# Output projection in three units, rotary in two operations, tables in 12, x from two queues: a two-layer encoder on one Trainium2 core

## The chip, the cores and the metric

The kernel runs on one core of one Trainium2 chip. The metric is the device time of one execution in microseconds (us), as the median over runs. The engines are TensorE (PE, matmuls and transposes, with a separate row PEld for its weight loads), VectorE (DVE), ScalarE (ACT), GpSimd (POOL) and SyncE (SP), which here only issues DMA transfers.

## What is computed

The reference, cut to the two layers that run (DEPTH is 2; SEQ is 512, D_MODEL 1024, 16 heads of 64, D_FF 4096):

```python
h = x
for i in range(DEPTH):
    y = rms_norm(h, norm1[i])
    y = mixer_a(y, ...) if i == 0 else mixer_b(y, ...)
    h = h + y
    h = h + jnp.square(jax.nn.relu(rms_norm(h, norm2[i]) @ w1[i])) @ w2[i]

def mixer_a(h, w_qkv, q_gain, k_gain, w_o, cos, sin):        # dilated attention
    qkv = (h @ w_qkv).reshape(B, S, 3, 3, 16, 64)            # 3 groups: dilation 1, 4, 16, radius 64, 64, 64
    for g in range(3):
        q = partial_rope(rms_norm(qkv[:, :, g, 0], q_gain[g]), cos, sin)   # rotary on 16 of 64 columns
        k = partial_rope(rms_norm(qkv[:, :, g, 1], k_gain[g]), cos, sin)
        num, den, mx = dilated_group(q, k, qkv[:, :, g, 2], dil, radius)
    ...                                                      # the groups are joined by their row maxima
    return (num / den) @ w_o

def mixer_b(h, w_in, conv_w, w_out):                         # gated convolution of width 3
    b, c, xt = split(h @ w_in); return (b * conv(c * xt)) @ w_out
```

## The kernel before

Every product is made in three matmuls: each float32 operand is split into a rounded high part and the remainder, and high x high, high x low and low x high are added in PSUM. A weight block of 128 rows (one k-block) is loaded by SP into `wraw` (4 buffers), ACT casts its high part `wh` (L292), POOL subtracts the remainder `wl` (L293; 6 buffers of each). The first two blocks of all are split by DVE (L959, L960).

The order of the work is written by a small planner. `add_unit` makes a unit of matmuls, cut into k-blocks; a clock counts its size, and one unit of that clock is the work of 12 matmuls of 512 columns. `at(pos, fn)` puts a task on a heap, and the run loop (L969 to L978) emits the tasks whose position has been passed between two matmuls. Each engine then runs its instructions in exactly that order, and waits at one hold up all behind it. For the attention the table `PLACES` gives the positions: its first row for pair 0, the second for pairs 1 to 6, the third for pair 7, the last.

**Start.** `setup` (L201) loads x into the tiles sm0 and sm12 (named sm in the profile), 128 columns by 128 columns at first and then 256 by 256, two transfers each (L198, L199), all issued by SP, with the weight blocks of the first four k-blocks between them. On ACT's queue stands the load of the norm gains (L203), then the table load and a first Exp (L214). `xT_fill` (L298) transposes x by PE (L301); ACT writes hgh, the high part with the gain applied (L305), and a copy to oT (L306), from which DVE makes the low part hgl (L307). PE's first matmul of the projection (L128) needs hgh of k-block 0. The copies of x transposed in oT go out to a DRAM buffer xs (L660).

**Layer 0, attention.** The 16 heads are 8 pairs. For each pair three units of 384 columns project q, k and v of the three groups. Two of them are evacuated to rawA and rawB (four tiles each, one for each residue r). Then come squares and sums (L364), the reciprocal root in ten small DVE operations (L367, L151 to L157), and `norm_mul` (L371): one multiplication by the root (L373) and the rotary in four operations (L379 to L382), on DVE or POOL as the table says. `qk_fill` transposes the result (L391) and splits it with the gains in `cols` (L405, L407). `tables` (L244) makes the cos and sin tables with the gains, tabA and tabB, in 48 small DVE operations (L254, L255) from loaded constants; `gain_cols` (L258) transposes the gain vectors to `cols` (L262, L263). Scores, softmax, the joining of groups by `spread` and `swap` (L428, L437), transposes (L520) and PV (L548) follow; ACT and DVE add both halves into oT (L551, L552).

**Output projection.** `split_o` splits oT into the tiles hgh and hgl of hgA. Two units of 512 columns (four tiles of 128 output columns each), over all eight k-blocks, are added to the trunk tiles hT, which `open_trunk` (L682) loads back from xs when the first tile is done; `wo_done` adds (L749), and `new_h` (L693) makes the high and low part for the next product (L705, L706) and the sum of squares (L707, L704). The last tile's oT is complete only after the last PV of pair 7; the last k-block of the first unit stands by itself, and its split at 1.0 units before that unit's end.

**The rest.** The MLP (L785), the gated convolution and a second MLP run with PE almost without a pause. The last additions of the last MLP (L817) go through a buffer zr (two of them), from which SP and ACT send the result out (L818, L819).

Of the kernel before, what the change touches and what calls it, by code (L numbers as in the profile page):

```python
# [11 lines left out]
F32 = mybir.dt.float32  # L12
# [23 lines left out]
def _constants():  # L36

    c = np.arange(128)
    r = np.arange(4)
    t = 4 * _C2M[:, None] + r[None, :]  # L40
    inv = (500000.0 ** (-np.arange(0, 16, 2) / 16.0)).astype(np.float32)
    ang = (t.astype(np.float32)[..., None] * inv).astype(np.float32).astype(np.float64)
    cos, sin = np.cos(ang), np.sin(ang)
    rope = np.concatenate([cos, cos, -sin, sin], axis=-1).astype(np.float32)
    m0 = np.zeros((128, 3, 256), np.float32)
    p = np.arange(128)
    for n, b in enumerate((0, 1, 3)):
        tq = 4 * _C2M[32 * b + p % 32] + p // 32
        tk = np.concatenate([4 * _C2M[_KEYC[j]] + _KEYR for j in ((b - 1, b) if b else (0, 3))])
        m0[:, n] = np.where(np.abs(tq[:, None] - tk[None, :]) <= 64, 0.0, BIG)  # L50
    m12 = np.zeros((128, 2, 128), np.float32)
    dm = _C2M[:, None] - _C2M[None, :]
    m12[:, 0] = np.where(np.abs(dm) <= 64, 0.0, BIG)
    m12[:, 1] = np.where(dm % 4 == 0, 0.0, BIG)
    return {"rope": rope.reshape(128, 4, 32), "m0": m0, "m12": m12.reshape(128, 256)}
# [7 lines left out]
         dN=0.04, P=11.9, dP=0.6, gP=0.5, lP=1.6, qA=0, qB=0, pA=0, pB=3, pN=2, vA=0, vB=8, xq=3.57, dxq=0.29, xs=6.25,  # L63
         lg=2.48, dlg=0.43, tb=5.8, dtb=0.3, gc=8.63),
# [10 lines left out]
def trunk_kernel(ctx, tc, x, norm1, norm2, wqkv, qgain, kgain, wo, win, conv, wout, w1, w2, c_rope, c_m0, c_m12, out):  # L75
# [119 lines left out]

    def load_x(lo, hi):
        dst = xtile[lo // 512][:, :, lo % 512:lo % 512 + hi - lo]
        sync.dma_start(dst[16:128], xr[0:112, :, lo:hi])  # L198
        sync.dma_start(dst[0:16], xr[112:128, :, lo:hi])  # L199

    def setup():  # L201
        vec = ptile(ab, [16, 128], F32, "vec", tag="tmpO")
        act.dma_start(vec, norm1.rearrange("l (k c) -> (l k) c", c=128))  # L203
# [10 lines left out]
        act.activation(small[:, 12:13], ident[:, 0:1], AF.Exp)  # L214
# [29 lines left out]
    def tables(ty):  # L244
        need("gains", 0, 3)
        mark("tables", 0)
        gb, rope = box["gb"], box["rope"]
        dst, w = (tabA, ty) if ty < 3 else (tabB, ty - 3)
        g = gb[:, ty % 2, ty // 2]
        for h in range(2):  # L250
            for a in range(2):
                s = slice(8 * a, 8 * a + 8)
                o = slice(8 * (1 - a), 8 * (1 - a) + 8)
                dve.tensor_mul(dst[:, 0, :, w, h, s], rope[:, :, s], g[:, None, s].to_broadcast([128, 4, 8]))  # L254
# [116 lines left out]
    def norm_mul(raw, stt, ng, tab, r, eng):  # L371
# [7 lines left out]
        eng.tensor_mul(t1[:, :ng], rot, tb[:, 0, r])  # L379
        eng.tensor_mul(t2[:, :ng, 0:8], v[:, :, 8:16], tb[:, 1, r, :, 0:8])  # L380
        eng.tensor_mul(t2[:, :ng, 8:16], v[:, :, 0:8], tb[:, 1, r, :, 8:16])
        eng.tensor_add(rot, t1[:, :ng], t2[:, :ng])  # L382

# [357 lines left out]

    def wo_done(half):
        def f(n, ps):
            if half == 0 and n == 0:
                for k in ("vp", "attn"):
                    close_pool(k)
                open_trunk()
            h = state["hT"][4 * half + n]
            dve.tensor_add(h, ps, h)  # L749
            new_h(4 * half + n, G2)  # L750
            if half == 1 and n == 3:
                for k in ("hgA", "oT", "psM0", "psG"):
                    close_pool(k)
                state["psM"] = open_pool("psM", space=PSUM, bufs=8)
        return f

# [28 lines left out]
    def mlp(layer, g_next, last):  # L785
# [18 lines left out]
        def u2_done(c, half):  # L804
            def f(n, ps):
# [9 lines left out]
                else:  # L815
                    o = ptile(state["tp"], [128, S], F32, "zr")
                    dve.tensor_add(o, ps, a)  # L817
# [184 lines left out]
```

## Time and profile before

| | us |
|---|---|
| Runs | 1516.8, 1513.8, 1516.64; median 1516.64 |
| Profiled execution: its time, its span | 1515.53, 1513.6 |
| Mean granted TensorE clock | 0.992 |
| Span of PE busy | 1483.0 (98%) |
| DVE, ACT, POOL busy | 706.4, 664.8, 716.4 |
| DMA moved | 144.77 MB, mean 96 GB/s |

A row of the profile's timeline has the start, the duration, the engine, the source line, the operation, what it writes and reads, its shape and count, and in brackets how long the engine was idle before it and what ended that. A row of the waits has the engine, the tile and line that waited, what ended the wait, then the total, the number and the longest. A row of the stretches has the busy time of PE, PEld, DVE, ACT and POOL, the granted clock, the DMA share and the rate.

### The profile page before, as it was taken

The numbers are of one execution on the slowest core, as the hardware profiler recorded it, in microseconds if no ns is written. First come the engines' busy times: TensorE is split into PE (matmuls) and PEld (weight loads), VectorE is DVE, ScalarE is ACT, GpSimd is POOL, SyncE is SP. The second block draws the span as 40 slices with busy tenths as digits, with TensorE's granted clock in tenths as the row PEclk, the third lists the DMA queues.
The fourth block names the chain that finished last, engine by engine and source line by source line (L and its number), as shares of the span: only waits on it lengthen the run. The fifth ranks groups of instructions, "written<-read, shape, count | busy, mean of one in ns | idle before, by whom it ended". The sixth has DMA issues, their size and how long they took to land.

```text
span 1513.6 us, 22622 instructions
## 1 busy us (share of the span) xinstructions
PE 1483.0 (98%) x7900; PEld 1293.4 (85%) x7900; DVE 706.4 (47%) x1553; ACT 664.8 (44%) x1364; POOL 716.4 (47%) x729
## 2 busy tenths in 40 slices
PE   9899999999999998999999999999999999999998
PEld 8799999999999987888888888888887888888887
DVE  4867767776767665643012223564447330122221
ACT  6456564556556564444333332433343443333320
POOL 4454444536354553554444445454454444444442
PEclk9899999999999999999999999999999999999999
DMA  6332322323132323222222232233332223222222
GB/s 151 126 112 63 102 79 86 91 75 102 53 115 60 102 84 127 103 98 96 99 97 98 91 103 96 81 90 99 98 111 84 98 92 102 97 96 94 99 90 84
DMA packets 163294, 144.77 MB, mean 96 GB/s; under 512 B 13748, under 2 KB 123116, under 8 KB 163180
## 3 DMA queue, kind: packets, MB, share of 16 engines
q1 hardware_dynamic: 162892, 143.06, 30.1%
q8 instruction: 62, 1.02, 0.3%
q14 instruction: 52, 0.43, 0.1%
q10 hardware_dynamic: 288, 0.27, 0.1%
HBM read 134.89 MB, written 8.39 MB: 95 GB/s over the span
## 4 chain that ended last, share of the span: by engine, by line
PE 77%; DVE 11%; issue 5%; POOL 3%; ACT 2%; DMA 1%; SPq 1%; POOLq 0%; ACTq 0%; DVEq 0%
PE g L128 72%; PE st L461 1%; PE o L548 1%; PE st L520 1%; PE st L391 1%; POOL wl L293 1%; DMA wraw<-in_a_wqkv 1%; DVE sm L451 1%; DVE rawA L373 1%; DVE ptl L293 1%; DVE stA L156 1%; DVE stA L155 1%; DVE sqa L704 1%; SPq L571 1%; ACT wh L292 0%
## 5 line engine op out<-in xcount | busy, mean ns | idle before, releaser
L293 POOL TENSOR_TENSOR wl<-wraw,wh 128x512 fp32r<-128x512 f32 (+1 forms) x542 | 638.2, 1198 | 712.2 <-ACT wh L292 701.2
L292 ACT CAST wh<-wraw 128x512 fp32r<-128x512 f32 (+1 forms) x542 | 300.8, 572 | 528.1 <-PE g L128 405.7
L128 PE MATMUL g<-hgBl,wh 128*128 128x512 f32 x704 | 274.8, 390 | 0.0
L128 PE MATMUL g<-hgBh,wl 128*128 128x512 f32 x704 | 274.6, 390 | 0.0
L128 PE MATMUL g<-hgBh,wh 128*128 128x512 f32 x704 | 274.6, 390 | 0.0
L128 PE MATMUL g<-wh,hgl 128*128 128x384 f32 x768 | 267.7, 349 | 0.5 <-DVE hgl L307 0.4
L128 PE MATMUL g<-wh,hgh 128*128 128x384 f32 x768 | 262.4, 342 | 1.6 <-DVE v L296 1.6
L128 PE MATMUL g<-wl,hgh 128*128 128x384 f32 x768 | 262.7, 342 | 0.0
L794 DVE SCALAR_TENSOR_TENSOR zr<-g,R 128x512 f32<-128x512 f32 x64 | 44.2, 691 | 293.4 <-PE g L128 293.3
L128 PEld LDWEIGHTS g<-hgBh,wl 128*128 128x128 f32 x704 | 132.7, 189 | 27.7
L128 PEld LDWEIGHTS g<-hgBh,wh 128*128 128x128 f32 x704 | 132.6, 188 | 27.9
L128 PEld LDWEIGHTS g<-hgBl,wh 128*128 128x128 f32 x704 | 132.7, 189 | 27.4
L128 PEld LDWEIGHTS g<-wh,hgl 128*128 128x128 f32 x768 | 145.3, 189 | 3.6 <-DVE hgl L307 1.6
L128 PEld LDWEIGHTS g<-wh,hgh 128*128 128x128 f32 x768 | 145.2, 189 | 2.7 <-DVE v L296 2.2
L128 PEld LDWEIGHTS g<-wl,hgh 128*128 128x128 f32 x768 | 144.9, 189 | 0.5
L811 DVE TENSOR_TENSOR acc<-g,acc 128x512 f32<-128x512 f32 x32 | 22.1, 692 | 138.2 <-PE g L128 138.2
L128 PE MATMUL g<-z0h,wh 128*128 128x512 f32 x192 | 74.7, 389 | 0.0
L128 PE MATMUL g<-z0l,wh 128*128 128x512 f32 x192 | 74.7, 389 | 0.0
L128 PE MATMUL g<-z0h,wl 128*128 128x512 f32 x192 | 74.7, 389 | 0.0
L470 ACT ACTIVATE sm<-sm,mxs 128x256 f32<-128x256 f32 x128 | 64.0, 501 | 15.1 <-DVE mxs L464 11.6
L292 ACT CAST pth<-st 128x512 fp32r<-128x512 f32 x64 | 37.6, 588 | 66.7 <-PE st L520 66.4
L293 DVE TENSOR_TENSOR ptl<-st,pth 128x512 fp32r<-128x512 f32 x64 | 43.5, 688 | 27.8 <-ACT pth L292 27.8
(222 smaller groups left out, 2379.0 us busy)
## 6 DMA issues: line engine op xcount, KB each, us to landing
wraw<-in_mlp_w SPq DMA_DIRECT2D x256, 256.0 KB
wraw<-in_a_wqkv SPq DMA_DIRECT2D x128, 128.0 KB
wraw<-in_a_wqkv SPq DMA_DIRECT2D x64, 192.0 KB
wraw<-in_a_wqkv SPq DMA_DIRECT2D x128, 64.0 KB
wraw<-in_b_win SPq DMA_DIRECT2D x64, 128.0 KB
v0d<-v SPq DMA_DIRECT2D x8, 512.0 KB
v<-v0d SPq DMA_DIRECT2D x64, 64.0 KB
wraw<-in_a_wo SPq DMA_DIRECT2D x16, 256.0 KB
```

The costliest lines, as they stand in the source:

```text
L128: pe.matmul(unit["ps"][n][:, :width], a, b, start=st, stop=sp)
L155: dve.tensor_mul(t, y, y)
L156: dve.scalar_tensor_tensor(t, t, -0.5, v, op0=ALU.mult, op1=ALU.mult)
L292: act.copy(hi, src)
L293: (eng or dve).tensor_sub(lo, src, f32(hi))
L373: dve.tensor_mul(v, v, stt[:, 2, ng * r:ng * r + ng, None].to_broadcast([128, ng, 64]))
L391: pe.transpose(o, raw[r][:, w, :], ident)
L451: dve.tensor_tensor_reduce(out=sm0[:, h, b], in0=ps[h][:, 256 * b2:256 * b2 + 256], in1=msk0[:, (0, 1, 1, 2)[b]], scale=1.0, scalar=3.0e38 ...
L461: pe.matmul(pv[:, :, g], a[:, 128 * r:128 * r + 128], k[:, 256 * r:256 * r + 256], start=(q == 0), stop=(q == 2))
L470: act.activation(t[:, h, b], t[:, h, b], AF.Exp, bias=mx(m)[:, c], scale=-1.0, accum_out=mx(d)[:, c])
L794: dve.scalar_tensor_tensor(zr, ps, 0.0, state["R"], op0=ALU.max, op1=ALU.mult)
L811: dve.tensor_add(a, ps, a)
```

## The change

x: `load_x` takes the queue as an argument. x(0:128) stays on SP, ahead of all; x(128:256), x(256:512) and x(512:768) go to ACT's queue, behind the norm gains and ahead of the table load; x(768:1024) stays on SP, behind the weight blocks. Tables: 12 operations of 128x8x16 instead of 48, with the constant in the order cos, cos, sin, -sin. Rotary: one multiplication for both tables into one tile with two planes, and one addition that reads the second plane with its halves swapped. In the first row of `PLACES` the constants and gains are loaded and turned into columns earlier; the third row is nearer to the second.

Output projection: the unit that comes first takes 384 columns (tiles 4 to 6) and k-blocks 0 to 6, and its sums are added to the trunk by `wo_rest`; then 512 columns (tiles 0 to 3) over all k-blocks, the last by itself; then the 384 columns again with k-block 7 alone; then 128 columns (tile 7) over all. The trunk has no tiles of its own: hT is oT, and x comes back into oT[k] from xs by `x_back(k)`, on SP, behind the split of k. In the last MLP two of four output tiles go through zz instead of zr.

```diff
-    def load_x(lo, hi):
+    def load_x(lo, hi, eng):
...
+        load_x(0, 128, sync)
         act.dma_start(vec, norm1.rearrange("l (k c) -> (l k) c", c=128))
-        load_x(0, 128)
+        load_x(128, 256, act)
         load_to(1)
-        load_x(128, 256)
+        load_x(256, 512, act)
         load_to(2)
-        load_x(256, 512)
+        load_x(512, 768, act)
         load_to(3)
-        load_x(512, 768)
+        load_x(768, 1024, sync)
         load_to(4)
-        load_x(768, 1024)
...
-            for a in range(2):
-                s = slice(8 * a, 8 * a + 8)
-                o = slice(8 * (1 - a), 8 * (1 - a) + 8)
-                dve.tensor_mul(dst[:, 0, :, w, h, s], rope[:, :, s], g[:, None, s].to_broadcast([128, 4, 8]))
-                dve.tensor_mul(dst[:, 1, :, w, h, s], rope[:, :, 16 + 8 * a:24 + 8 * a],
-                               g[:, None, o].to_broadcast([128, 4, 8]))
+            dve.tensor_mul(dst[:, :, :, w, h], rope.rearrange("p r (s c) -> p s r c", s=2),
+                           g[:, None, None, :].to_broadcast([128, 2, 4, 16]))
...
-        t1 = ptile(ab, [128, 8, 16], F32, "tmpR1" + of, bufs=2)
-        t2 = ptile(ab, [128, 8, 16], F32, "tmpR2" + of, bufs=2)
+        t = ptile(ab, [128, 2, 8, 16], F32, "tmpR" + of, bufs=2)
...
-        eng.tensor_mul(t1[:, :ng], rot, tb[:, 0, r])
-        eng.tensor_mul(t2[:, :ng, 0:8], v[:, :, 8:16], tb[:, 1, r, :, 0:8])
-        eng.tensor_mul(t2[:, :ng, 8:16], v[:, :, 0:8], tb[:, 1, r, :, 8:16])
-        eng.tensor_add(rot, t1[:, :ng], t2[:, :ng])
+        eng.tensor_mul(t[:, :, :ng], rot[:, None].to_broadcast([128, 2, ng, 16]), tb[:, :, r])
+        t1, t2 = (t[:, i, :ng].rearrange("p n (a d) -> p n a d", a=2) for i in range(2))
+        eng.tensor_add(rot.rearrange("p n (a d) -> p n a d", a=2), t1, t2[:, :, ::-1])
...
-        state["hT"] = [ptile(hp, [128, S], F32, f"hT{k}") for k in range(KT)]
+        state["hT"] = oT
...
-        for k in range(KT):
-            sync.dma_start(state["hT"][k], xs[k])
...
+    def wo_rest(n, ps):
+        dve.tensor_add(oT[4 + n], ps, oT[4 + n])
...
+    def x_back(k):
+        sync.dma_start(oT[k], xs[k])
+
     for k in range(KT - 1):
         at(clock[0] - 1.5 + 0.5 * k, lambda k=k: split_o(k))
+        at(clock[0] - 0.3 + 0.5 * k, lambda k=k: x_back(k))
     sm_o = sm_T(lambda kt: hgA[kt])
-    add_unit(512, ld_plain(wo[0], 0), sm_o, 4, ps_g, 512, wo_done(0), kblocks=((0, 1), (2, 3), (4, 5), (6,), (7,)))
-    at(clock[0] - 1.0, lambda: split_o(KT - 1))
-    add_unit(512, ld_plain(wo[0], 512), sm_o, 4, ps_w1, 512, wo_done(1))
+    add_unit(384, ld_plain(wo[0], 512, 384), sm_o, 3, ps_g, 512, wo_rest, kblocks=((0, 1), (2, 3), (4, 5), (6,)))
+    add_unit(512, ld_plain(wo[0], 0), sm_o, 4, ps_g, 512, wo_done, kblocks=((0, 1), (2, 3), (4, 5), (6,), (7,)))
+    at(clock[0] - 2.0, lambda: split_o(KT - 1))
+    at(clock[0] - 0.3, lambda: x_back(KT - 1))
+    add_unit(384, ld_plain(wo[0], 512, 384), sm_o, 3, ps_w1, 512, lambda n, ps: wo_done(4 + n, ps), kblocks=((7,),))
+    add_unit(128, ld_plain(wo[0], 896, 128), sm_o, 1, lambda n: ps_w1(3), 512, lambda n, ps: wo_done(7, ps))
...
-                    o = ptile(state["tp"], [128, S], F32, "zr")
+                    o = ptile(state["tp"], [128, S], F32, "zr" if n < 2 else "zz")
```

In the third row of `PLACES` mulA goes from 1.1 to 1.79, pA (rotary tiles of the first half on POOL) from 3 to 0, pB from 3 to 1, S12 from 6.0 to 6.5, W from 8.0 to 9.0 and P from 9.8 to 11.1, and four others with them; in the first row dlg goes from 0.43 to 0.36 and gc from 8.63 to 7.2. After line 228 the lines of the changed kernel stand 3 to 8 above those of before.

On ACT, at the start of the program, this stood before (in and out by name, with their shape):

```order
L203 DMA vec<-in_norm 16x128
L214 ACT_TABLE_LOAD
L214 ACTIVATE small<-ident 128x1
L305 ACTIVATE hgh_85<-st,cols 128x512
L306 COPY oT_74<-st 128x512
```

and now, with the semaphores that an instruction waits for (sm0 is x(0:512), sm12 is x(512:1024); DMAHW6 is raised by the transfer in the third row from the top, the first of x(256:512); DMAHW0, at its second turn, by the first transfer of the second weight block):

```order
L198 DMA sm0_130<-in_x 112x4x128
L199 DMA sm0_130<-in_x 16x4x128
L198 DMA sm0_130<-in_x 112x4x256
L199 DMA sm0_130<-in_x 16x4x256 [waits DMAHW3_49]
L198 DMA sm12_131<-in_x 112x4x256 [waits DMAHW6_49]
L199 DMA sm12_131<-in_x 16x4x256 [waits DMAHW0_49]
L214 ACT_TABLE_LOAD
L214 ACTIVATE small_70<-ident_65 128x1 [waits Pool_49]
L301 ACTIVATE hgh0_85<-st_203,cols_66 128x512 [waits DVE_49,PE_49]
```

Six transfers have moved ahead of the table load on ACT; none was there.

On DVE, ahead of pair 0's reciprocal root (the row with small), before:

```order
L364 TENSOR_REDUCE stA<-sqq 128x6 x2
L254 TENSOR_TENSOR tabB<-rope,gb 128x4x8
L255 TENSOR_TENSOR tabB<-rope,gb 128x4x8
...
L254 TENSOR_TENSOR tabB<-rope,gb 128x4x8
L255 TENSOR_TENSOR tabB<-rope,gb 128x4x8
L367 SCALAR_TENSOR_TENSOR stA<-stA,small 128x24
```

and now:

```order
L360 TENSOR_REDUCE stA<-sqq 128x6
L259 COPY cols<-st 128x46
L261 MEMSET cols 16x6 x2
L262 TENSOR_SCALAR cols<-cols 128x3
L360 TENSOR_REDUCE stA<-sqq 128x6
L251 TENSOR_TENSOR tabB<-rope,gb 128x8x16 x2
L363 SCALAR_TENSOR_TENSOR stA<-stA,small 128x24
```

Two table operations stand between the last sum and the root instead of eight, and the copy of the gains to cols has moved from behind the root to ahead of it.

On PE, behind the last PV of the last pair (the rows with o; hgh_99 and hgl_100 are the split of oT's tile 7, lower numbers those of earlier tiles), before:

```order
L548 MATMUL o<-ptl,v 64x128
L548 MATMUL o<-pth,v 64x128
L128 MATMUL g<-hgh_99,wh 128x512
L128 MATMUL g<-hgl_100,wh 128x512
L128 MATMUL g<-hgh_99,wl 128x512
```

and now:

```order
L542 MATMUL o<-ptl,v 64x128
L542 MATMUL o<-pth,v 64x128
L128 MATMUL g<-hgh_93,wl 128x512
L128 MATMUL g<-hgh_95,wh 128x512
L128 MATMUL g<-hgl_96,wh 128x512
L128 MATMUL g<-hgh_95,wl 128x512
L128 MATMUL g<-hgh_97,wh 128x512
...
L128 MATMUL g<-hgh_97,wl 128x512
L128 MATMUL g<-hgh_99,wh 128x512
L128 MATMUL g<-hgl_100,wh 128x512
```

Sixteen matmuls on tiles 4, 5 and 6 stand between the last PV and the first use of tile 7, where there were none.

More of the change, by code (lines that the diff above doesn't have):

```diff
@@ L43, in _constants @@
     cos, sin = np.cos(ang), np.sin(ang)
-    rope = np.concatenate([cos, cos, -sin, sin], axis=-1).astype(np.float32)
+    rope = np.concatenate([cos, cos, sin, -sin], axis=-1).astype(np.float32)
     m0 = np.zeros((128, 3, 256), np.float32)
@@ L63 @@
          dN=0.04, P=11.9, dP=0.6, gP=0.5, lP=1.6, qA=0, qB=0, pA=0, pB=3, pN=2, vA=0, vB=8, xq=3.57, dxq=0.29, xs=6.25,
-         lg=2.48, dlg=0.43, tb=5.8, dtb=0.3, gc=8.63),
+         lg=2.48, dlg=0.36, tb=5.8, dtb=0.3, gc=7.2),
     dict(sqA=0.02, rsA=0.87, mulA=1.79, dmA=0.28, TA=4.8, dT=0.19, sqB=0.17, rsB=0.8, mulB=1.07, dmB=0.12, TB=4.05, S0=0.45,
@@ L67 @@
          dN=0.04, P=10.9, dP=0.64, gP=0.9, lP=1.6, qA=0, qB=0, pA=0, pB=3, pN=2, vA=0, vB=12),
-    dict(sqA=0.02, rsA=0.8, mulA=1.1, dmA=0.5, TA=4.5, dT=0.1, sqB=0.17, rsB=0.8, mulB=1.07, dmB=0.12, TB=4.05, S0=0.45,
-         dS=0.55, E0=1.1, X=3.1, lX=1.0, S12=6.0, dS12=0.24, E12=6.5, dE12=0.18, W=8.0, lW=0.3, lF=1.0, N0=9.4, N12=8.4,
-         dN=0.03, P=9.8, dP=0.34, gP=0.15, lP=0.6, qA=0, qB=0, pA=3, pB=3, pN=2, vA=0, vB=9),
+    dict(sqA=0.02, rsA=0.87, mulA=1.79, dmA=0.28, TA=4.8, dT=0.19, sqB=0.17, rsB=0.8, mulB=1.07, dmB=0.12, TB=4.15, S0=0.45,
+         dS=0.55, E0=1.1, X=3.1, lX=0.6, S12=6.5, dS12=0.24, E12=7.1, dE12=0.2, W=9.0, lW=0.4, lF=1.0, N0=10.5, N12=9.55,
+         dN=0.04, P=11.1, dP=0.56, gP=0.45, lP=1.4, qA=0, qB=0, pA=0, pB=1, pN=2, vA=0, vB=9),
 ]
@@ L194, in trunk_kernel @@
              sm12.rearrange("p h b c -> p (h b c)").rearrange("p (r c) -> p r c", r=4)]
-    def load_x(lo, hi):
+    def load_x(lo, hi, eng):
         dst = xtile[lo // 512][:, :, lo % 512:lo % 512 + hi - lo]
-        sync.dma_start(dst[16:128], xr[0:112, :, lo:hi])
-        sync.dma_start(dst[0:16], xr[112:128, :, lo:hi])
+        eng.dma_start(dst[16:128], xr[0:112, :, lo:hi])
+        eng.dma_start(dst[0:16], xr[112:128, :, lo:hi])
     def setup():
         vec = ptile(ab, [16, 128], F32, "vec", tag="tmpO")
+        load_x(0, 128, sync)
         act.dma_start(vec, norm1.rearrange("l (k c) -> (l k) c", c=128))
-        load_x(0, 128)
+        load_x(128, 256, act)
         load_to(1)
-        load_x(128, 256)
+        load_x(256, 512, act)
         load_to(2)
-        load_x(256, 512)
+        load_x(512, 768, act)
         load_to(3)
-        load_x(512, 768)
+        load_x(768, 1024, sync)
         load_to(4)
-        load_x(768, 1024)
         make_identity(nc, ident)
@@ L230, in load_gains @@
         if i == 0:
-            box["gb"] = ptile(ab, [128, 2, 3, 16], F32, "gb", tag="tmpR1", bufs=2)
-            box["rope"] = ptile(ab, [128, 4, 32], F32, "rope", tag="tmpR2", bufs=2)
+            box["gb"] = ptile(ab, [128, 2, 3, 16], F32, "gb", tag="tmpR", bufs=2)
+            box["rope"] = ptile(ab, [128, 4, 32], F32, "rope", tag="tmpR", bufs=2)
             box["v"] = ptile(ab, [64, 128], F32, "vec2", tag="tmpO")
@@ L739, in sm_T, with wo_done @@
         return f
[L742 to L755, printed above, removed]
+    def wo_rest(n, ps):
+        dve.tensor_add(oT[4 + n], ps, oT[4 + n])
+    def wo_done(n, ps):
+        if n == 0:
+            for k in ("vp", "attn"):
+                close_pool(k)
+            open_trunk()
+        dve.tensor_add(oT[n], ps, oT[n])
+        new_h(n, G2)
+        if n == 7:
+            for k in ("hgA", "psM0", "psG"):
+                close_pool(k)
+            state["psM"] = open_pool("psM", space=PSUM, bufs=8)
     def ps_w1(n):
```

## The prediction

> **What bounds the kernel now.** I read the page's list of engines first, then the waits of TensorE, then the busy time of the engines in stretches, and last the timeline at the places where these three point.
>
> ```profile
> PE 1483.0 (98%) x7900; PEld 1293.4 (85%) x7900; DVE 706.4 (47%) x1553; ACT 664.8 (44%) x1364; POOL 716.4 (47%) x729
> ```
>
> TensorE (PE) is busy for 98% of the span, and its matmuls are the same in number and shape after the change. So only three things can move the time: PE's idle time, time at half clock (which counts as busy), and what lies ahead of the first and behind the last matmul. The waits name what ended PE's idle time (us in total, times, longest).
>
> ```profile
> PE st L391 <- DVE cols L263: 3.5, 1, 3.5
> PE st L437 <- DVE spread L428: 3.0, 7, 1.4
> PE st L391 <- DVE rawA L382: 2.9, 3, 1.3
> PE g L128 <- ACT hgh L292: 2.0, 1, 2.0
> PE st L391 <- DVE k1l L407: 1.6, 1, 1.6
> PE o L548 <- DVE oT L552: 1.5, 5, 0.6
> PE st L301 <- DMA sm<-in_x: 1.4, 1, 1.4
> PE st L391 <- POOL rawB L382: 0.8, 1, 0.8
> PE st L520 <- DVE sm L508: 0.6, 1, 0.6
> PE g L128 <- DVE hgl L293: 0.6, 1, 0.6
> ```
>
> The stretches show where they lie (columns: length, then PE, PEld, DVE, ACT and POOL busy, granted clock, DMA share, GB/s).
>
> ```profile
> 0.00:40.00 40.00, 36.79 (x206) 33.93 (x207) 20.03 (x72) 24.43 (x56) 17.41 (x27) 1.00 0.62 159
> 40.00:80.00 40.00, 33.58 (x200) 31.11 (x199) 31.51 (x97) 19.12 (x48) 19.95 (x28) 0.87 0.38 119
> 560.00:600.00 40.00, 35.30 (x229) 29.44 (x229) 25.66 (x55) 21.14 (x49) 18.16 (x19) 1.00 0.30 95
> 600.00:640.00 40.00, 40.00 (x168) 32.28 (x167) 24.23 (x31) 18.03 (x30) 18.77 (x13) 0.96 0.38 132
> 720.00:760.00 40.00, 40.00 (x178) 33.14 (x177) 0.00 (x0) 13.02 (x22) 18.32 (x16) 1.00 0.27 92
> ```
>
> The MLP (720 to 760) has no idle time at all, so nothing can be won in it. The three places with idle time are the start (3.2 us), pair 0 (6.4 us, and a clock of 0.87) and the last pair with the hand-over to the output projection (4.7 us, and 0.96 behind it). The change touches all three, and the tail.
>
> **The start.** ScalarE's (ACT) queue is the point.
>
> ```profile
> 0.72 0.38 ACTq L203 DMA_DIRECT2D vec<-in_norm  x1
> 1.14 1.28 ACT L214 ACT_TABLE_LOAD   x1 [1.14 <-PEq L990]
> 2.43 0.20 ACT L214 ACTIVATE small<-ident 128x1 f32<-128x1 f32 x1
> 5.47 0.69 ACT L305 ACTIVATE hgh<-st,cols 128x512 fp32r<-128x512 f32 x1 [2.83 <-PE st L301]
> 5.72 0.57 SPq L198 DMA_DIRECT2D sm<-in_x  x1
> 6.34 0.62 SPq L199 DMA_DIRECT2D sm<-in_x  x1
> 6.39 0.42 PE L128 MATMUL g<-wh,hgh 128*128 128x384 f32 x1
> 11.21 0.63 PE L301 MATMUL st<-ident,sm 128*128 128x128 f32 x4 [1.39 <-DMA sm<-in_x]
> ```
>
> Before, SyncE (SP) issues x(256:512) at 5.72, and its first transpose starts at 11.21, after PE has waited 1.39 for the landing. With the change ACT issues six x transfers of 0.57 to 0.62 us ahead of the table load. The order of the instructions (in the section on the change) shows that the issue of x(512:768) waits for a semaphore that the landing of x(256:512) raises. So the table load, the first Exp and the first hgh, which the first matmul needs, stand behind a landing. x(256:512) is now issued at 0.72 + 0.38 + 0.57 + 0.62 and gaps, about 2.4. Before, it landed 11.21 - 5.72 = 5.5 us after its issue, which would be 7.9 now; fewer bytes stand ahead of it, but x(128:256) and the first weights are under way with it. I take 8.5, between 7 and 10. Then follow 0.57 + 0.62 of issues, 1.28, 0.20, 0.69 and 0.23 from hgh to matmul (5.47 + 0.69 to 6.39) and 0.2 of gaps: the first matmul starts at 12.3 instead of 6.39, +5.9. Against this the wait of 1.4 goes, since x(256:512) has landed by then, and 0.4 of smaller waits (0 to 40 has 3.2 idle). PE, warm from its transposes, now idles for some five us. The row of 600 to 640 prices a stall: a clock of 0.96 is 40 x 0.04 = 1.6 us lost; the row of 40 to 80 bounds it at 40 x 0.13 = 5.2, much of which falls on idle time. I take +1.6. Sum of the start: 5.9 - 1.4 - 0.4 + 1.6 = **+5.7**, between 0 and +9.
>
> The Trainium skill (DMA: Bandwidth & Descriptors, Issuing engines are not separate DMA queues) says that transfers interleave on the same 16 engines whichever engine issued them, and that a second issuer saves only issue time. By that, x(256:512) would end with all that is asked for by then (x(0:512), 1.05 MB, and two weight blocks of 0.2), 9.1 us at the 159 GB/s of the first row above, at 9.8 as an estimate, and the sum would come out 1.3 higher; 5.72 to 11.21, with one issuer, leaves this open.
>
> **Pair 0.** Its rotary is late because VectorE (DVE) comes late to the reciprocal root.
>
> ```profile
> 41.24 1.01 DVE L254 TENSOR_TENSOR tabB<-rope,gb 128x32 f32<-128x32 f32 x1
> 44.32 0.17 DVE L367 SCALAR_TENSOR_TENSOR stA<-stA,small 128x24 f32<-128x24 f32 x1
> 40.15 4.10 POOL L293 TENSOR_TENSOR wl<-wraw,wh 128x384 fp32r<-128x384 f32 x4 [4.21 <-ACT wh L292]
> 50.56 0.26 DVE L379 TENSOR_TENSOR tmpR<-rawA,tabA 128x96 f32<-128x96 f32 x1
> 51.09 0.26 DVE L382 TENSOR_TENSOR rawA<-tmpR,tmpR 128x96 f32<-128x96 f32 x1
> 55.50 0.26 DVE L382 TENSOR_TENSOR rawA<-tmpR,tmpR 128x96 f32<-128x96 f32 x1
> ```
>
> While GpSimd (POOL) makes its weight remainders back to back (40.15 to 44.25), every other small DVE operation takes about 1.0 instead of 0.17, and the last eight table operations, which fall there, hold the root's first operation (L367) from 41.24 to 44.32. With 12 table operations instead of 48 only two stand there, which makes L367 some 2.5 us earlier. But the ten small operations behind it then fall deeper into POOL's burst, where one or two more of them cost 0.8 each: about 1.2 of the 2.5 is left. The rotary goes from four operations to two: 50.56 to 51.09 and 0.18 more is 0.71 for each of four r; one product of twice the width and one addition should take about 0.55, so 4 x 0.16 = 0.6. The copy of the gains to cols with its memsets, which stands between r = 0 and r = 1 and in PE's longest wait (3.5), goes ahead of the chain: 0.4 saved. With 0.4 for half clock that falls away: 1.2 + 0.6 + 0.4 + 0.4 = **-2.6**, between -1 and -5. The last rotary, now at 55.50, should come at about 53. PE now asks for the gain vectors 3.9 us earlier (gc 8.63 to 7.2, at 2.7 us a unit of the plan, 12 matmuls of 0.225), and they are loaded 1.5 earlier; if the SP queue holds them up, PE waits for up to 0.8, which the range has.
>
> **Pairs 1 to 6.** Of the waits, 1.6 for spread (3.0 less the longest) and 1.5 for the last addition into oT are spread over the pairs. Shorter rotary operations on DVE and POOL free some of it. Half: **-1.6**, between 0 and -3. Where POOL, not DVE, is the limit, nothing is won.
>
> **Last pair and hand-over.** Before, three matmuls of the last k-block come right behind the last PV, and PE waits through the copy, the addition and the split.
>
> ```profile
> 596.13 0.58 ACT L551 COPY tmpO<-o 64x512 f32<-64x512 f32 x1 [2.76 <-PE o L548]
> 596.75 0.69 DVE L552 TENSOR_TENSOR oT<-o,tmpO 64x512 f32<-64x512 f32 x1 [2.65 <-ACT tmpO L551]
> 597.47 0.62 ACT L292 CAST hgh<-oT 128x512 fp32r<-128x512 f32 x1 [0.23 <-DVE oT L552]
> 598.14 0.49 PE L128 MATMUL g<-hgh,wh 128*128 128x512 f32 x1 [2.04 <-ACT hgh L292]
> 600.91 0.63 PE L128 MATMUL g<-hgh,wh 128*128 128x512 f32 x1
> 602.38 1.35 DVE L749 TENSOR_TENSOR hT<-g,hT 128x512 f32<-128x512 f32 x2 [3.25 <-DMA hT<-xs]
> 1508.31 0.39 PE L128 MATMUL g<-wh,z1l 128*128 128x512 f32 x1
> ```
>
> After the change 16 matmuls that don't need the last tile stand there. At 40 / 178 = 0.225 apart (720 to 760) they take 3.6 us, and the chain's 2.0 + 0.6 fits under them with 1.0 to spare; if that cover were gone, 2.6 would come back. The extra matmuls come from the 384-column unit that is started early, which also fills the gaps of the last pair's chain, whose places are relaxed to nearly those of the other pairs. Removed: rawB 0.8, k1l 1.6, spread 1.4, oT 0.6, sm 0.6, hgh 2.0, hgl 0.6, and the half clock, which the duration 0.63 against 0.39 shows, 0.24 x 7 = 1.7: 9.3 in all. A pair like the others still waits for about 1.1. That gives -8.2. Against it stands DVE: seven of the eight tiles come out within 5 us instead of in two halves of four, and each brings an addition, a remainder and a sum of squares of about 0.69 each, some 15 us of DVE. The first MLP unit takes 12 x 0.225 = 2.7 us for a k-block, so DVE's 2.1 a tile keeps up, but the last addition frees a PSUM bank 1 to 2 us after PE asks for it. I price the hand-over at +1, between 0 and +3 (nearest row: 40.00 of 40.00 busy at 600 to 640, where nothing waits now). The trunk tiles are the attention's output tiles, so x comes back by a DMA behind each split; they are issued a few us ahead of the additions, where before DVE waited 3.25 for them beside a busy PE. Sum **-7.2**, between -3 and -9.
>
> The Trainium skill (TensorE: Matmul & The Clock Gate, What's actually happening) puts half clock after a wholly idle window of about 3.4 us. By that, idle times of 2.04 and 0.55 would have cost no clock and the term would be -5.5. The 0.96 and the 0.63 show that they did, so I keep -7.2.
>
> **Tail.** Before, the last addition waits for a transfer of its buffer.
>
> ```profile
> 1509.35 0.69 DVE L817 TENSOR_TENSOR zr<-g,acc 128x512 f32<-128x512 f32 x1 [0.66 <-DMA out<-zr]
> ```
>
> PE ends at 1508.31 + 0.39 = 1508.70. With two buffers more the addition starts at 1508.75: **-0.6**. What follows it (landing of out) is unchanged.
>
> **The sum.** 5.7 - 2.6 - 1.6 - 7.2 - 0.6 = -6.3. The profiled execution took 1515.53 (span 1513.6), so 1509.2; the median of the runs is 1516.64, 1.1 more. I predict 1509.5. About 0.2%, or 3 us, can be told from no change in this kernel: faster means below 1513.6, slower above 1519.7.
>
> **The rivals.** *The start costs nothing* (x(256:512) lands by 5, or the issues don't wait): then the first matmul comes by 7 and the wait at 11.21 is gone; -12 in place of -6.3, about 1503.5. For it: in the first 2.4 us little else is asked for. Against: before, the landing took 5.5 us. Chance 0.17. *DVE's backlog at the MLP takes the hand-over's gain*: half of -8.2 comes back, as PE waits 4 us for PSUM or for the sums; 1513. For it: 15 us of DVE operations behind one another, each open to POOL's 0.8. Against: the 128-column unit's 24 matmuls (5.4 us) stand ahead of the MLP. Chance 0.17. *ACT's queue is held for long* (slower): x(0:768) and four weight blocks are 2.3 MB. Were x(256:512) served last, at the 159 GB/s of 0 to 40, it would land at 17 and the first matmul come at 21, which eats the whole gain (1518); at the 110 GB/s that the transfers ran at from 20 to 24 it would be 23 and 27, and the time 1524. It makes the kernel slower from a first matmul at 22.5 us on. Against it: 252 GB/s from 8 to 12.
>
> ```profile
> 8.00:12.00 4.00, 2.62 (x16) 2.17 (x15) 1.58 (x3) 0.58 (x2) 0.00 (x0) 1.00 1.10 252
> 20.00:24.00 4.00, 3.90 (x24) 3.61 (x23) 1.73 (x2) 3.54 (x8) 3.79 (x6) 1.00 0.48 110
> ```
>
> Chance 0.08. For the forecast 0.58 is left.
>
> **How the numbers follow.** 1509.5 is the likeliest case. Its own range, with the start from 0 to +9 and the end from -3 to -9 not both at their ends, is 1504 to 1514. The 8-in-10 range reaches down into the free start and up to the backlog: 1501 to 1516. Faster: 0.58 x 0.93 + 0.17 + 0.17 x 0.35 = 0.77; slower 0.08; within 0.2% the rest, 0.15.
>
> **What would show it.** Right: the table load at 9 to 10 us and the first 384-wide matmul near 12.3, with half clock behind it; no idle time over 0.5 us after the last PV and a clock of 1.00 from 600 to 640; rawA's last rotary at about 53; the last addition at PE's end. Wrong: a table load at 2 to 5 us (then the start is free), PE waiting for PSUM or sums in the MLP's first unit, or a first matmul later than 20.

## The result and the profile after

The changed kernel is slower: 1529.20 us median of 6 runs (1527.73 to 1533.58) against 1516.43 of 6 (1513.47 to 1516.98) for the kernel before; ratio 1.0094, 95% interval 1.0077 to 1.0111, or +12.8 us where -7 was forecast. The profiled execution of the changed kernel took 1533.58 (span 1531.8), 4.4 above its median, so that its places below lie a little too far apart.

The waits of PE in the profile after (engine, tile and line; what ended the wait; total, times, longest):

```profile
PE st L514 <- POOL sm L500: 9.0, 2, 7.8
PE st L431 <- DVE spread L422: 8.7, 7, 3.9
PE g L709 <- ACT sgh L288: 4.7, 2, 3.3
PE g L128 <- ACT hgh L301: 4.6, 1, 4.6
PE st L385 <- DVE rawA L376: 4.4, 4, 2.0
...
PE g L128 <- POOL wl L289: 1.1, 3, 0.7
...
PE g L128 <- ACT wh L288: 0.9, 1, 0.9
```

The stretches after, with the columns as before:

```profile
0.00:40.00 40.00, 32.72 (x174) 30.84 (x175) 12.62 (x29) 22.82 (x52) 15.84 (x26) 1.00 0.56 136
40.00:80.00 40.00, 35.60 (x207) 33.50 (x206) 33.14 (x91) 18.07 (x45) 18.48 (x21) 0.91 0.42 129
560.00:600.00 40.00, 31.60 (x155) 26.69 (x154) 24.54 (x53) 19.86 (x46) 17.14 (x19) 0.84 0.45 137
600.00:640.00 40.00, 38.18 (x211) 30.60 (x210) 19.80 (x30) 17.94 (x36) 10.27 (x12) 0.97 0.13 37
640.00:680.00 40.00, 37.90 (x153) 29.82 (x153) 21.91 (x25) 16.51 (x28) 23.65 (x18) 0.94 0.36 114
```

The waits that the change was to remove at the end of the attention (k1l, rawB, hgh of the split) are gone from the list. In their place stand a wait of 7.8 for POOL, one of 3.9 for spread, new ones for weights (wh, wl) at 634 to 642, and one of 1.4 for the sums behind the hand-over (of the 4.7 for sgh, 3.3 belong to a later place and were there before). The stretch of 600 to 640 has a DMA share of 0.13 where there was 0.38, and 640 to 680 is no longer full.

A way to find where time goes is to read, in each timeline, when PE starts the same piece of work (us):

| PE starts | before | after | p_x | p_rot | p_wo | w_places | w_rot | w_places_pack |
|---|---|---|---|---|---|---|---|---|
| first 384-wide matmul | 6.39 | 12.56 | 12.67 | 6.79 | 6.02 | 5.84 | 6.27 | 5.95 |
| first swap (spread) of pair 0 | 73.87 | 77.69 | 78.04 | 70.88 | 73.31 | 73.05 | 73.45 | 73.32 |
| first swap of pair 7 | 553.92 | 557.93 | 559.79 | 547.48 | 557.64 | 554.32 | 551.92 | 553.69 |
| second swap of pair 7 | 575.87 | 584.43 | 581.74 | 569.41 | 584.00 | 576.39 | 576.97 | 574.36 |
| MLP's first matmul | 625.82 | 639.67 | 630.09 | 619.31 | 638.56 | 627.96 | 630.00 | 621.37 |
| first matmul on z0 | 713.36 | 732.85 | 717.65 | 706.85 | 731.13 | 720.94 | 720.99 | 713.01 |
| last matmul | 1508.31 | 1527.10 | 1511.95 | 1502.05 | 1525.23 | 1514.83 | 1515.30 | 1507.27 |

Before against after: +6.2 at the start, of which pair 0 and pairs 1 to 6 give back all but 2.2 by the second swap of pair 6 (506.67 and 508.84); then the last pair and the hand-over lose 17.3, to +19.5 at z0; from there to the last matmul (+18.8) little changes.

The start after, in the timeline (ACTq is ACT's queue of transfers):

```profile
2.55 0.62 ACTq L198 DMA_DIRECT2D sm<-in_x  x1
...
9.15 0.58 ACTq L198 DMA_DIRECT2D sm<-in_x  x1
...
10.43 1.28 ACT L214 ACT_TABLE_LOAD   x1 [10.43 <-DMA sm<-in_x]
11.73 0.20 ACT L214 ACTIVATE small<-ident 128x1 f32<-128x1 f32 x1
11.84 0.67 ACT L301 ACTIVATE hgh<-st,cols 128x512 fp32r<-128x512 f32 x1
...
12.56 0.69 PE L128 MATMUL g<-wh,hgh 128*128 128x384 f32 x1 [4.55 <-ACT hgh L301]
...
14.54 0.52 PE L128 MATMUL g<-wh,hgh 128*128 128x384 f32 x1
```

The issue of x(512:768) waited until 9.15, the table load came at 10.43 and the first matmul at 12.56. The matmuls behind it last 0.52 instead of 0.34 and start 0.32 apart instead of 0.17. That is half clock, although the column of the clock says 1.00 for this stretch.

The last pair after:

```profile
573.43 0.42 SPq L342 DMA_DIRECT2D v0d<-v  x1
...
579.21 4.48 SPq L347 DMA_DIRECT2D v<-v0d  x8
...
583.73 0.93 SPq L766 DMA_DIRECT2D oT<-xs  x2
...
584.76 1.02 SPq L723 DMA_DIRECT2D wraw<-in_a_wo  x2
...
586.58 2.08 SPq L766 DMA_DIRECT2D oT<-xs  x3
...
591.34 1.27 ACT L288 CAST wh<-wraw 128x512 fp32r<-128x512 f32 x2 [9.90 <-DMA wraw<-in_a_wo]
...
592.04 2.49 POOL L289 TENSOR_TENSOR wl<-wraw,wh 128x512 fp32r<-128x512 f32 x2 [6.11 <-ACT wh L288]
...
592.67 0.69 DVE L737 TENSOR_TENSOR oT<-g,oT 128x512 f32<-128x512 f32 x1 [5.61 <-DMA oT<-xs]
...
594.50 1.89 POOL L500 TENSOR_SCALAR sm<-sm,mxs 128x256 f32<-128x256 f32 x4
```

These rows read as a chain. SP sends v out at 573.43 and waits for it until 579.21; eight loads of v and two of x follow, and only then, at 584.76, two weight blocks, with three more loads of x behind them on the same DMA engines. ACT stands for 9.90 on these weights, POOL's remainders behind ACT, and the last four of POOL's normalisations, which PE's transposes need, behind the remainders (594.50). On DVE the last normalisation stands behind an addition that waits 5.61 for x from xs.

### The profile page after: what moved, and what is told of

It is laid out like the page before. It is cut to its first block, busy times and chain, and to the rows that moved or that the text cites. A ratio compares the mean times of both kernels' runs of the same rounds, so it can differ in the third digit from the quotient of the medians.

```text
span 1531.8 us, 22499 instructions
## 1 busy us (share of the span) xinstructions
PE 1488.8 (97%) x7900; PEld 1300.8 (85%) x7900; DVE 706.7 (46%) x1456; ACT 664.0 (43%) x1372; POOL 704.8 (46%) x673
## 4 chain that ended last, share of the span: by engine, by line
PE 83%; DVE 10%; DMA 2%; issue 2%; ACT 1%; POOL 1%; SPq 0%; ACTq 0%; POOLq 0%
PE g L128 76%; PE o L542 2%; PE st L514 2%; PE st L385 1%; PE st L455 1%; DVE rawB L369 1%; DVE sm L445 1%; DVE stB L360 1%; DVE tmpR L374 1%; DVE sqa L696 1%; POOL wl L289 1%; DVE hgBl L698 0%; DMA sm<-in_x 0%; DMA wraw<-in_a_wo 0%; DVE oT L546 0%
## 5 line engine op out<-in xcount | busy, mean ns | idle before, releaser
L289 POOL TENSOR_TENSOR wl<-wraw,wh 128x512 fp32r<-128x512 f32 (+2 forms) x550 | 641.8, 1188 | 748.4 <-ACT wh L288 720.6
L288 ACT CAST wh<-wraw 128x512 fp32r<-128x512 f32 (+2 forms) x550 | 301.3, 565 | 534.1 <-PE g L128 407.9
L464 ACT ACTIVATE sm<-sm,mxs 128x256 f32<-128x256 f32 x128 | 63.6, 498 | 14.8 <-DVE mxs L458 11.3
```

The costliest lines, as they stand in the source:

```text
L288: act.copy(hi, src)
L289: (eng or dve).tensor_sub(lo, src, f32(hi))
L464: act.activation(t[:, h, b], t[:, h, b], AF.Exp, bias=mx(m)[:, c], scale=-1.0, accum_out=mx(d)[:, c])
```

## The experiments

The runs were measured in four groups, each with the kernel before on the same chip; the times are medians, differences and ratios are against it, ratios with their 95% intervals. By these intervals one difference is uncertain by about 2 us, and what one run has more or less than another by 3 to 4. Theory A: the start and the pairs did what was forecast, and the loss lies in the output projection's part of the change. Rivals: the late start or the new rotary brings the last pair into a worse phase.

### The change in four parts

**p_x**: of the diff only `load_x` and `setup`.

> The kernel before with only x loaded by two queues. Theory A (the loss lies in the output projection and the last pair; the start costs what the trace of the changed kernel shows, a first matmul at 12.6 instead of 6.4): +4 to +7 us against before, 1520 to 1523. Rival B (the later start is taken up by pair 0's wait for VectorE, which is idle meanwhile): within 2 us of before.

1520.04 against 1515.08: +5.0, ratio 1.0033 (1.0021 to 1.0044). ACT's queue in its timeline:

```profile
9.22 0.61 ACTq L198 DMA_DIRECT2D sm<-in_x  x1
9.88 0.63 ACTq L199 DMA_DIRECT2D sm<-in_x  x1
10.54 1.28 ACT L214 ACT_TABLE_LOAD   x1 [10.54 <-DMA sm<-in_x]
```

The first matmul comes at 12.67, and the start's loss is not taken up by pair 0: +4.2 at its first swap. Rival B falls.

**p_rot**: only the tables, `norm_mul`, the constant, dlg and gc.

> The kernel before with only the tables in 12 operations, the rotary in two, and the constants and gains earlier. Theory A: pair 0 gains 2 to 3 us and pairs 1 to 6 together 1 to 2: -3 to -5 us, about 1512. Rival C (the wide rotary operation makes VectorE collide with GpSimd in the other pairs, where the wait for spread has grown from 0.3 to 0.8 us): 0 to +3.

1508.32: -6.8, ratio 0.9956 (0.9940 to 0.9971), more than the 3 to 5 that were expected. By the table 3.0 are won at pair 0's first swap and 6.4 by pair 7's. Its waits of PE:

```profile
PE st L431 <- DVE spread L422: 6.2, 7, 1.4
PE st L385 <- DVE rawA L376: 4.3, 4, 2.0
```

The wait for spread has doubled (3.0 before), and still the kernel is faster. Rival C, which read that growth as a loss, falls. From pair 0's first swap to pair 7's PE's listed waits are even longer (6.4 in all, 5.1 before). What became shorter there is PE's busy time, 473.8 to 470.2; its transposes of rawB account for 1.5 of that (14.7 to 13.2), and where the rest comes from stays open.

**p_wo**: only `PLACES[2]`, `open_trunk`, `wo_rest`, `wo_done`, `x_back` and the four units.

> The kernel before with only the output projection in three units, the trunk in the attention's output tiles and the relaxed places of the last pair. Theory A: the whole loss of the last pair and the hand-over, +12 to +18 us, about 1530. Rival B (the loss comes with the shifted start or the new rotary, which bring the last pair's steps into another phase): +0 to +5.

1531.14: +16.1, ratio 1.0103 (1.0088 to 1.0118). The whole loss, without the shifted start and the new rotary.

**p_rest**: all the rest of the change.

> The changed kernel with the output projection, the trunk and the last pair's places as before (x by two queues, tables and rotary, output tiles). Theory A: +6 for the start, -4 for pairs, -0.6 for the tail: 0 to +3 us, about 1518. Rival B: 1525 or more.

1514.80: -0.3, ratio 0.9991 (0.9982 to 1.0000). The results agree within their noise: 5.0 - 6.8 + 16.1 = 14.3, less about half a us for the tail, against 12.8; and p_rest, expected at 0 to +3, lies 2 above 5.0 - 6.8 less the tail.

### What in the output projection costs

All these are p_wo with one or two edits; its own difference to before is +16.1.

**w_noback**:

```diff
-        at(clock[0] - 0.3 + 0.5 * k, lambda k=k: x_back(k))
...
-    at(clock[0] - 0.3, lambda: x_back(KT - 1))
```

> Only the output projection's change, and of it the eight transfers that bring x back into oT are left out, so the residual x is missing from the sum and the attention's own output is added in its place. Theory A1 (the loads from xs stand in SP's queue ahead of the weight blocks and share the DMA engines with them; ACT and POOL then wait for the weights with the last pair's normalisation behind them): 6 to 10 us faster than p_wo, 1521 to 1525, and no wait for POOL over 2 us at the last pair's transposes. Theory A2 (the narrow last unit drains the weight buffers) and A3 (the relaxed places): within 2 us of p_wo.

1527.93 against 1514.80: +13.1, ratio 1.0089 (1.0074 to 1.0104). 3.0 less than p_wo, at most half of what A1 expected and no more than the uncertainty. PE's wait for POOL is 4.0 instead of 7.4, where A1 had under 2. DVE's wait for x is gone, but ACT still waits for the weights, which SP issues behind the loads of v, until 587.70 instead of 590.56:

```profile
587.70 1.27 ACT L292 CAST wh<-wraw 128x512 fp32r<-128x512 f32 x2 [6.18 <-DMA wraw<-in_a_wo]
```

**w_pack**: the last unit's weights in blocks of four k-blocks side by side; sm_7 takes them apart, and mult=4 has the planner's clock count 12 matmuls a block.

```diff
-    add_unit(128, ld_plain(wo[0], 896, 128), sm_o, 1, ...)
+    def ld_7(raw, kt):
+        sync.dma_start(raw.rearrange("p (q c) -> p q c", q=4),
+                       wo[0][512 * kt:512 * kt + 512, 896:1024].rearrange("(q p) c -> p q c", q=4))
+    add_unit(512, ld_7, sm_7, 1, ..., kblocks=((0,), (1,)), mult=4)
```

> Only the output projection's change, but the weights of its last 128 columns come in two blocks of 128x512 (four k-blocks side by side) instead of eight of 128x128, so that a buffer holds 12 matmuls instead of 3. Theory A2: 4 to 6 us faster than p_wo, 1525 to 1527, with the waits for wh and wl at the MLP's start gone; the 7.4 us wait for POOL before the last PV stays. Theories A1 and A3: within 2 us of p_wo.

1525.47: +10.7, ratio 1.0073 (1.0056 to 1.0089), 5.4 less than p_wo, as A2 expected. The waits for wh and wl are gone; of the hand-over these are left in its waits from 600 to 720:

```profile
PE g L715 <- ACT sgh L292: 1.4, 1, 1.4
PE g L716 <- DVE sgl L293: 0.5, 1, 0.5
```

**w_noback_pack**: both.

> Both of these: the residual left out and the last 128 columns packed. Theories A1 and A2 together: 11 to 16 us faster than p_wo, within 5 us of the kernel before, 1515 to 1520. If the relaxed places cost much (A3): 1524 or more.

1522.21: +7.4, ratio 1.0054 (1.0038 to 1.0070). 8.7 less than p_wo, between the two expectations: the two add (3.0 + 5.4), and a large part is left.

**w_places**: p_wo with the third row of `PLACES` as before.

> Only the output projection's change, with the last pair's places as before. Theory A3 (the relaxed places, with the rotary of the last pair on VectorE instead of GpSimd, delay the chain): 4 to 10 us faster than p_wo. Theory A1: within 3 us of p_wo, since the order of SP's queue is the same.

1519.41: +4.6, ratio 1.0029 (1.0017 to 1.0040). 11.5 less than p_wo, more than expected and the largest of all single edits, with the transfers as they were. Its waits of PE on the same tiles:

```profile
PE st L437 <- DVE spread L428: 1.6, 6, 0.3
PE st L391 <- DVE k1l L407: 1.6, 1, 1.6
...
PE st L520 <- POOL sm L506: 0.2, 1, 0.2
```

The long waits for spread and for POOL are gone. POOL makes the normalisations ahead of the remainders of the late weights here:

```profile
579.85 1.94 POOL L506 TENSOR_SCALAR sm<-sm,mxs 128x256 f32<-128x256 f32 x4
586.76 2.54 POOL L293 TENSOR_TENSOR wl<-wraw,wh 128x512 fp32r<-128x512 f32 x2 [4.97 <-ACT wh L292]
```

A1 alone, as stated, falls: the transfers made PE wait for POOL where the normalisations stand behind the weights that they delay. Whether they cost anything beside that is not shown, since no run leaves them out with the places as before.

**w_places_pack**: both edits.

> Only the output projection's change, with the last pair's places as before and the last 128 columns packed into two blocks. If the two causes add as single effects (11.7 us from the places, 5.7 from the narrow unit): 1513 to 1515, about the kernel before. If both are one queue's shortage and the second only gets worse when the first is gone, or the x loads take over: 1518 or more.

1515.74 against 1515.50: +0.2, ratio 1.0000 (0.9991 to 1.0009). -15.9 against p_wo, close to the sum of 11.5 and 5.4, and a little above the 1513 to 1515 that were expected. In the table its MLP starts at 621.37, 4.4 earlier than before, and its z0 at 713.01, 0.4 earlier: the hand-over eats 4.1. DVE works through the additions, remainders and sums of squares almost without a pause from 611.77 to 629.97, and only then can ACT (630.03) cast the sums that PE waits for. From 600 to 640 it has lost PE time and clock where the kernel before had 40.00:

```profile
600.00:640.00 40.00, 38.08 (x157) 30.24 (x156) 26.43 (x34) 17.99 (x31) 18.92 (x14) 0.96 0.33 98
```

### How the places cost

**w_pn**: p_wo with pN=4 in the third row, so that the last pair's normalisations are all on DVE.

> p_wo with all eight normalisations of the last pair on VectorE, none on GpSimd. If GpSimd's order (normalisations behind the remainders of weights that come late) alone makes the 7.4 us wait: it goes, 6 to 9 us faster than p_wo. If VectorE, which waits 5.3 us for x from xs with its last normalisation behind that, stands just as late: 1 to 3 us faster only.

1527.25 against 1516.00: +11.3, ratio 1.0073 (1.0053 to 1.0093), 4.8 less than p_wo, between the two expectations. The wait for POOL is gone, and one of 3.1 for an addition behind x from xs has come in its place.

**w_noback_pn**: the same with w_noback.

> w_noback (residual left out) with all eight normalisations on VectorE. If the wait has both causes, the weights on GpSimd's side and x from xs on VectorE's: both are gone, the remaining wait of 4.7 us and its half clock vanish, 5 to 8 us faster than w_noback, about 1521. If it is something else in the chain: within 2 us of w_noback.

1523.49: +7.5, ratio 1.0053 (1.0037 to 1.0069), 5.6 less than w_noback, as the first expectation had it. Both causes hold: weights on POOL's side, x on DVE's.

**w_rot**: p_wo with the last pair's rotary at its places of before.

```diff
-         rsA=0.87, mulA=1.79, dmA=0.28, TA=4.8, dT=0.19, TB=4.15, pA=0, pB=1
+         rsA=0.8,  mulA=1.1,  dmA=0.5,  TA=4.5, dT=0.1,  TB=4.05, pA=3, pB=3
```

> p_wo with the last pair's rotary at its places of before (earlier, three of four tiles of each half on GpSimd), all later places relaxed as in the change. If the places cost by the rotary on VectorE: the wait for spread of 4.6 us shrinks to 1.4 and the time falls by 2 to 4 us; the 7.4 us wait stays. If the rotary's places make no difference, within 1 us of p_wo.

1522.99: +7.0, ratio 1.0051 (1.0035 to 1.0066), 9.1 less than p_wo where 2 to 4 were expected. Its waits of PE:

```profile
PE st L520 <- POOL sm L506: 7.3, 2, 6.6
PE st L437 <- DVE spread L428: 1.6, 6, 0.3
```

The wait for spread of 4.6 is gone; in the table the first swap of pair 7 comes 5.7 earlier than in p_wo (551.92 against 557.64), and the second 7.0. The rows of the changed kernel show why spread was late:

```profile
552.26 4.34 POOL L289 TENSOR_TENSOR wl<-wraw,wh 128x384 fp32r<-128x384 f32 x4
...
553.75 1.04 DVE L374 TENSOR_TENSOR tmpR<-rawB,tabB 128x192 f32<-128x192 f32 x1
...
557.62 0.25 DVE L422 TENSOR_TENSOR spread<-mxs,quad 128x64 f32<-128x64 f32 x1
```

With pB=1 DVE has three rotary tiles of the second half instead of one, ahead of spread, while POOL, free of them, starts its remainders; beside these a DVE operation takes 1.04 that takes 0.36 otherwise. The positions of that half (mulB, dmB) are the same in both rows of the table, so this wait comes from pB. But the edit puts back eight numbers, out of 21 that the change altered in this row (the section on the change counts ten), and what the other seven add to the 9.1 was not run by itself.

The wait for POOL stays at 6.6. So the rotary's places are the larger part; the chain's later positions have 11.5 - 9.1 = 2.4, which is within the uncertainty, although the wait of 6.6 goes with them (0.2 in w_places). By the table w_places wins 2.0 on w_rot at the MLP's first matmul and nothing at z0.

### The start, and versions without the loss

**x_fix**: p_x with the identity, the table load and the first Exp ahead of ACT's x transfers, and x(512:768) on SP.

> The kernel before with x(128:512) on ACT's queue, but the table load and the first Exp ahead of these transfers and x(512:1024) on SP. If the loss of p_x is ACT's table load behind a landing: the first matmul comes at 6.4 to 8 again and the time is within 2 us of before. If two queues as such slow the first x or the first weights (the same DMA engines): first matmul at 9 or later, +3 to +5 as in p_x.

1521.83 against 1515.50: +6.3, ratio 1.0045 (1.0030 to 1.0060). The first matmul comes at 14.37, later still, and the loss is above both expectations.

```profile
8.84 0.58 ACTq L198 DMA_DIRECT2D sm<-in_x  x1
...
12.95 0.58 ACTq L199 DMA_DIRECT2D sm<-in_x  x1
13.63 0.69 ACT L305 ACTIVATE hgh<-st,cols 128x512 fp32r<-128x512 f32 x1 [10.96 <-DMA sm<-in_x]
...
14.37 0.69 PE L128 MATMUL g<-wh,hgh 128*128 128x384 f32 x1 [8.08 <-ACT hgh L305]
```

The table load was early, but two issues on ACT waited until 8.84 and 12.95, with hgh behind them. So the table load was only the first in line behind the held queue.

**x_fix2**: p_x with only x(128:256) on ACT.

> The kernel before with only x(128:256) on ACT's queue, which needs no semaphore there, and the rest on SP. If the loss of p_x and x_fix is ACT's queue standing behind a transfer's semaphore: the first matmul comes at 6.4 to 7 and the time is 0 to 2 us below before. If any x on ACT's queue slows the start: first matmul at 9 or later and +3 or more.

1516.30 against 1516.00: +0.3, ratio 1.0003 (0.9994 to 1.0013). No issue on ACT waits, and the loss is gone:

```profile
1.88 0.64 ACTq L199 DMA_DIRECT2D sm<-in_x  x1
...
2.55 1.28 ACT L214 ACT_TABLE_LOAD   x1 [2.55 <-issue]
```

Its first matmul is at 7.94, above the 6.4 to 7 that were expected: x(0:128) lands later beside x(128:256). Nothing is won either.

**best1**: before with p_rot's edits and zr and zz.

> Of the change only the tables, the rotary, the earlier gains and the output tiles zr and zz; x from SP alone and the output projection as before. Theory A: the sum of its parts, -6.8 from p_rot and -0.6 from the tail: 1507 to 1509, faster than both kernels.

1508.28 against 1515.50: -7.2, ratio 0.9951 (0.9939 to 0.9964), faster than both kernels. Against p_rot (-6.8) the tail's 0.6 can't be told apart.

**best2**: best1 with the edits of w_places_pack.

> best1 with the output projection in three units, the last pair's places as before and the last 128 columns packed. If the places and the narrow unit cost what the single runs showed, it is 1 to 2 us faster than best1, about 1506; if VectorE's backlog at the MLP's start or the transfers of x back weigh more, 3 to 6 us slower than best1.

1508.32: -7.2, ratio 0.9954 (0.9942 to 0.9967). The same as best1, between the two expectations, so that the mended output projection neither wins nor loses.

## Why the prediction was wrong, point by point

**The start** (+5.7 forecast) was right in mechanism and size: first matmul 12.56 where 12.3 stood, x(256:512) landed by 9.15 where 8.5 stood, half clock behind it; p_x measures +5.0. The reason was right as well, but wider than stated: in x_fix the table load was out of the way, and the held issues delayed hgh all the same. The rivals of a free start and of a queue held to 20 us did not happen.

**Pair 0** (-2.6) and **pairs 1 to 6** (-1.6): p_rot gained 3.0 and 3.4. That the first is near its forecast is partly luck, since its terms were off both ways. In p_rot the root's first operation came 3.0 earlier (41.37 against 44.32; 2.5 forecast), the small operations from there to the first rotary took 0.8 less (1.3 more was forecast), and from the first rotary to the last 0.3 was lost (1.0 to be won). For three of four r the rotary takes 0.56 (57.03 to 57.59) in the changed kernel, where 0.55 was forecast, but the first r falls beside POOL's remainders and takes 1.93 (53.37 to 55.30):

```profile
53.37 1.04 DVE L374 TENSOR_TENSOR tmpR<-rawA,tabA 128x192 f32<-128x192 f32 x1
54.44 0.93 DVE L376 TENSOR_TENSOR rawA<-tmpR 128x96 f32<-128x96 f32 x1
...
57.03 0.36 DVE L374 TENSOR_TENSOR tmpR<-rawA,tabA 128x192 f32<-128x192 f32 x1
57.42 0.26 DVE L376 TENSOR_TENSOR rawA<-tmpR 128x96 f32<-128x96 f32 x1
57.59 0.55 DVE L369 TENSOR_TENSOR rawA<-rawA,stA 128x384 f32<-128x384 f32 x1
```

The term of pairs 1 to 6 was sized at half, and its reason failed: the waits for spread, which were to shrink, went from 1.6 to 4.8 between the first swaps of pair 0 and pair 7, and those for oT only from 1.5 to 0.9.

**Tail** (-0.6): the last addition starts 0.04 behind the end of the last matmul (1527.10 + 0.39), as forecast. No run has the tail by itself.

```profile
1527.53 0.69 DVE L818 TENSOR_TENSOR zz<-g,acc 128x512 f32<-128x512 f32 x1 [0.67 <-PE g L128]
```

**Last pair and hand-over** (-7.2) is the step that failed; p_wo measures +16.1. Three statements in it were wrong, and one number was misread: the oT 0.6 among the waits to be removed lies between 250 and 350 us, in the pairs before, and stands in the term of pairs 1 to 6 as well.
- "Whose places are relaxed to nearly those of the other pairs": the term counted the waits that this takes away. But the same table row takes most of the last pair's rotary from POOL and gives it to DVE, which then works beside POOL's remainders; the wait of 1.4 for spread at the second swap went, and one of 3.9 came at the first, where there was none. w_rot measures 9.1 for the rotary's places and engines together. The wait for spread comes from pB, which the prediction did not cost.
- "They are issued a few us ahead of the additions": the issues of x from xs, and the later places, were held against the additions alone, and not against what they are moved past in SP's queue and what waits behind the weights on ACT and POOL. The longest wait for POOL's normalisation is 7.8 now; before it was 0.2. w_noback measures 3.0 for the transfers, which is not clear of the uncertainty; w_pn (4.8) and w_noback_pn (5.6) are clear of it and show both ends of the chain.
- The 128-column unit was priced only as cover for the hand-over (5.4 us of matmuls). Each of its weight blocks takes a whole buffer for three matmuls, so six buffers hold 18 matmuls, 4 us as an estimate at 0.225 each, and weights come late: PE waits 0.9, 0.7 and 0.2 within this unit and 0.2 behind the MLP's first matmul, at half clock from 638 to 641.6. w_pack measures 5.4.

The hand-over itself was sized at +1, between 0 and +3; w_places_pack has 4.1, with PE waiting for the sums (1.4 and 0.5) at half clock. That is the rival of DVE's backlog, at its own price of 4, though the waits for the sums are only 1.9 of it and half clock (40 x 0.04 = 1.6) most of the rest. Where the other errors are mended (w_places_pack) PE does reach the MLP 4.4 earlier, about half of the 8.2, with the waits for hgh and hgl gone as the cover of 16 matmuls promised, and the hand-over takes it back. The slower rival had the wrong place: it looked for the loss at the start.

Of the signs, those of the start (the table load 0.4 late) and the tail came true. Those of the end did not: the clock from 600 to 640 is 0.97, and behind the last PV PE waits up to 1.4, among others for the sums in the MLP's first unit, which was a sign of being wrong. The last rotary came at 58.57, not 53: that sign left the late start out (52.05 in p_rot, which starts on time).

## What to carry to other kernels

When a step is moved or a unit is cut narrower, follow every in-order queue that it passes: what is issued behind it, which weights that delays, and which later step of another kind stands behind the work on those weights. Buffers count in blocks, but cover counts in matmuls, so a narrow unit runs itself and the start of its successor out of weights. A table of positions is a change of its own, to be costed number by number like code, and a wait that grows is not by itself a loss: in p_rot the wait for spread doubled and the kernel was 6.8 us faster.

## What the runs showed of the hardware

A transfer issued on ACT's queue stood for 3.5 us for the landing of another (5.67 to 9.15 in the changed kernel; 9.42 to 12.95 in x_fix), and all of ACT's work with it. Two issuing queues brought x no earlier: with x(128:256) on ACT, x(0:128) landed at least 1.2 later (its first transpose came at 5.50 after a wait of 1.11 for it, instead of at 4.32 without one), and the time was the same (x_fix2, 1.0003). Small DVE operations beside POOL's remainders took 0.93 to 1.04 where they take 0.26 to 0.36 otherwise (53.37 to 55.30 and 57.03 to 57.59 in the changed kernel). The column of the granted clock showed 1.00 in the first 40 us of the changed kernel while matmuls of 384 columns took 0.52 instead of 0.34 from 13 to 17 us; in p_x, with the same durations, it showed 0.57 from 12 to 16. Durations tell what that column can miss.
